# In both expert layers, every block of the first product from block 36 on runs as 512-column matmuls, where every second one did

## The chip, the cores and the metric

The kernel runs on one core of one Trainium2 chip. The metric is the device time of one execution in microseconds (us), the median over several runs. Engines are named as in the profile: PE is TensorE's matmul, PEld its weight load, DVE is VectorE, ACT is ScalarE, POOL is GpSimd, SP is SyncE.

## The reference

A model of three layers, on 256 tokens of width 1024, in float32: a layer of retention and a layer of differential attention, each followed by an expert layer (`peer_ffn`), and then a third layer with a gated recurrence and two feed-forward parts. The change touches the two expert layers only. For a token, 8 heads choose 16 experts each out of 16384 by two sets of 128 keys; of each chosen expert a row of `u` is multiplied with the token, and the weighted gelu of it with a row of `v`:

```python
u_e = jnp.take(u, idx, axis=0)
v_e = jnp.take(v, idx, axis=0)
act = jax.nn.gelu(jnp.einsum('ted,td->te', u_e, xc).astype(jnp.float32))
return jnp.einsum('te,ted->td', (gate * act).astype(v_e.dtype), v_e)
```

## The kernel before

The kernel doesn't gather experts. `peer` computes the first product for all 16384 of them, in 128 blocks (`i2`) of 128 experts by 256 tokens, takes gelu of it into a tile H, multiplies H with gates that are zero but for the chosen experts, and multiplies H with all of `v`. It runs twice, once a layer.

Products are made exact enough by splitting: each operand becomes a high and a low float32r half, and three of the four products are summed. Of x the two halves lie side by side in one tile, `both`, with 256 columns each. Weights come by DMA on SP's queue in pieces of 128 x 1024 (`stream`), four in flight, and `split` turns a piece into `wh` (ScalarE, line 124) and `wl` (VectorE, line 125), with three buffers of each and high priority. So for every block ScalarE and VectorE do one long split, about two blocks ahead of its use.

There are two ways to compute a block. `gemm_a` makes 24 matmuls of 256 columns (lines 146 to 148): for each of 8 slices of the width, high weights by high x, high weights by low x, low weights by high x, all into the same 256 columns of a PSUM bank. `gemm_ab` makes 16 (lines 158 to 162): high weights by both halves of x at once, 512 columns, and low weights by high x, 256 columns. That leaves two partial results side by side in the bank. ScalarE copies the right one to `lo` (line 1246), VectorE adds the two into `su` (line 1247), and gelu then reads `su` instead of the bank. `lo` and `su` lie in `parts`, a tile with two places for each.

PSUM has eight banks here: two for blocks (`s.mm`), two for transposes and scores (`s.aux`), four for gates (`s.acc`). So a block can start when the block before the last one has left its bank.

Blocks 0 to 35 (`K0` is 36) run beside the routing, which VectorE does; they all use `gemm_a`. From block 36 on the gates are made as well, 64 groups of 4 tokens spread over the blocks: VectorE builds two one-hot tiles for a group (lines 1452 and 1453; the second is written into one of two places, so it waits for the group before the last one), PE multiplies them in 8 short f16 matmuls (line 1464), and VectorE and ScalarE apply the result to H (lines 1469 and 1472). Once gates have been applied to some tokens, the gelu of later blocks goes to a tile of its own for these tokens, and VectorE multiplies it into H (lines 1260 and 1261). From block 36 on even blocks use `gemm_ab` and odd blocks `gemm_a`.

Nobody writes the order of the instructions on an engine by hand: a planner orders them before the run by readiness and priority over the whole program, and each engine then follows its list strictly in that order.

After block 127 the second product follows: for each `i2` ScalarE and VectorE split a row of H into `gh` and `gl`, and PE multiplies (line 1286).

Of the kernel before, what the change touches and what calls it, by code (L numbers as in the profile page):

```python
# [49 lines left out]
K0 = 36  # L50
# [17 lines left out]
class Ker:  # L68
# [1095 lines left out]
    def peer(s, l, xs, units_q, units_u, units_v, ln):  # L1164
        nc, A = s.nc, s.A
        with ExitStack() as cx:
# [14 lines left out]
            parts = xs[0].rearrange("p (b a t) -> p b a t", b=2, a=2)  # L1181
# [34 lines left out]
            def scores(c):  # L1216
                ps = s.aux()[:, :T].rearrange("p (a b) -> p a b", a=2)
                for tt in range(2):
                    nc.tensor.matmul(ps[:, tt], qT[:, c, tt * 128:tt * 128 + 128], sk[:, c], start=True, stop=True)
                nc.scalar.activation(sc[:, :, c], ps, AF.Copy)  # L1220
# [15 lines left out]
            pend = []  # L1236
            for i2 in range(NKEYS):
                ps = s.mm()
                if i2 < K0 or i2 % 2:
                    ps = ps[:, :T]  # L1240
                    s.gemm_a(next(units_u), xT, ps)
                else:

                    s.gemm_ab(next(units_u), both, ps)
                    lo, su = (parts[:, i2 // 2 % 2, j] for j in range(2))
                    nc.scalar.activation(lo, ps[:, T:], AF.Copy)
                    nc.vector.tensor_tensor(su, ps[:, :T], lo, op=ALU.add)
                    ps = su
                if i2 < 2:
                    if i2 == 0:  # L1250
                        scores(15)
                    s.route_keys(rt, sc, 14 + i2)
                nt = 4 * g
                if nt == 0:
                    nc.scalar.activation(H[:, i2], ps, AF.Gelu_apprx_tanh)
                else:
                    if nt < T:
                        nc.scalar.activation(H[:, i2, nt:], ps[:, nt:], AF.Gelu_apprx_tanh)
                    ge = po.tile([128, T], F32, name="gelu")
                    nc.scalar.activation(ge[:, :nt], ps[:, :nt], AF.Gelu_apprx_tanh)  # L1260
                    nc.vector.tensor_tensor(H[:, i2, :nt], H[:, i2, :nt], ge[:, :nt], op=ALU.mult)
                if 2 <= i2 < K0:
                    for _ in range(ROUTE_STEPS):
                        next(route, None)
                    if i2 == K0 - 1:
                        for _ in route:
                            pass
                elif i2 >= K0:
                    for f in pend:
                        f(i2 + 1)  # L1270
                        g += 1
                    e = (i2 + 2 - K0) * (T // 4) // (NKEYS - KEND - K0)
                    pend = [s.gates(H, s.onehots(po, rt, j), j) for j in range(g, min(e, T // 4))]
# [391 lines left out]
```

## Time and profile before

| | |
|---|---|
| median of 3 runs | 2709.18 us (2705.35 to 2709.56) |
| the profiled execution, its time | 2703.24 us |
| the profiled execution, its span | 2701.4 us |
| mean granted TensorE clock | 0.996 |
| PE busy | 2660.6 us (98%) |
| PEld busy | 2326.7 us (86%) |
| DVE busy | 1955.8 us (72%) |
| ACT busy | 1427.8 us (53%) |

The profile shows one execution. Its span goes from the first to the last instruction; its time is measured from outside and is 1.8 us longer. Busy shares are of the span. Matmuls overlap and their ends are modelled, so the share of PE says little by itself; the starts of matmuls are what can be relied on.

### The profile page before, as it was taken

The numbers are of one execution on the slowest core, as the hardware profiler recorded it, in microseconds if no ns is written. First come the engines' busy times: TensorE is split into PE (matmuls) and PEld (weight loads), VectorE is DVE, ScalarE is ACT, GpSimd is POOL, SyncE is SP. The second block draws the span as 40 slices with busy tenths as digits, with TensorE's granted clock in tenths as the row PEclk, the third lists the DMA queues.
The fourth block names the chain that finished last, engine by engine and source line by source line (L and its number), as shares of the span: only waits on it lengthen the run. The fifth ranks groups of instructions, "written<-read, shape, count | busy, mean of one in ns | idle before, by whom it ended". The sixth has DMA issues, their size and how long they took to land. (4 is left out here: it accounts for less than half of the span.)

```text
span 2701.4 us, 43500 instructions
## 1 busy us (share of the span) xinstructions
PE 2660.6 (98%) x16326; PEld 2326.7 (86%) x16326; DVE 1955.8 (72%) x3668; ACT 1427.8 (53%) x2553; POOL 12.3 (0%) x32
## 2 busy tenths in 40 slices
PE   9999999999999999999999999999999999999999
PEld 7789999999888888799999998888878887888887
DVE  7558978888666668689788886666687576665774
ACT  4445555555555555555555555555555474443554
POOL 0000000000000000000000000000000000000000
PEclk9999999999999999999999999999999999999999
DMA  6455555545666664355555556565655543122554
GB/s 211 153 185 183 180 172 168 168 165 190 200 194 195 193 195 151 102 181 179 174 165 166 169 179 210 192 193 194 195 169 189 188 161 110 56 71 78 172 187 148
DMA packets 125570, 454.65 MB, mean 168 GB/s; under 512 B 14464, under 2 KB 15248, under 8 KB 125104
## 3 DMA queue, kind: packets, MB, share of 16 engines
q1 hardware_dynamic: 124064, 447.62, 50.9%
q0 software_dynamic: 1152, 4.19, 0.4%
q8 instruction: 128, 2.10, 0.3%
q14 instruction: 82, 0.67, 0.1%
q10 hardware_dynamic: 144, 0.07, 0.0%
HBM read 448.66 MB, written 3.15 MB: 167 GB/s over the span
## 5 line engine op out<-in xcount | busy, mean ns | idle before, releaser
L125 DVE TENSOR_TENSOR wl<-raw,wh 128x1024 fp32r<-128x1024 f32 x830 | 1014.5, 1223 | 429.2 <-ACT wh L124 427.5
L124 ACT ACTIVATE wh<-raw 128x1024 fp32r<-128x1024 f32 x830 | 879.4, 1060 | 736.0 <-issue 198.9
L146 PE MATMUL mm<-xT,wh 128*128 128x256 f32 x1648 | 468.7, 285 | 3.2 <-ACT ge L258 2.3
L148 PE MATMUL mm<-xT,wl 128*128 128x256 f32 x1648 | 465.8, 283 | 1.8 <-DVE wl L125 1.8
L147 PE MATMUL mm<-xT,wh 128*128 128x256 f32 x1648 | 467.1, 284 | 0.0
L158 PE MATMUL mm<-xT,wh 128*128 128x512 f32 x1050 | 381.0, 402 | 0.8 <-ACT wh L124 0.6
L147 PEld LDWEIGHTS mm<-xT,wh 128*128 128x128 f32 x1648 | 314.6, 191 | 5.0 <-DVE xT L260 0.3
L146 PEld LDWEIGHTS mm<-xT,wh 128*128 128x128 f32 x1648 | 314.2, 191 | 5.4 <-ACT ge L258 2.7
L1286 PE MATMUL acc<-wl,gh 128*128 128x512 f32 x1024 | 317.4, 389 | 0.3
L148 PEld LDWEIGHTS mm<-xT,wl 128*128 128x128 f32 x1648 | 314.7, 191 | 2.6 <-DVE wl L125 2.4
L1286 PE MATMUL acc<-wh,gl 128*128 128x512 f32 x1024 | 316.6, 389 | 0.0
L159 PE MATMUL mm<-xT,wl 128*128 128x256 f32 x1050 | 292.5, 279 | 0.8 <-DVE wl L125 0.8
L1286 PE MATMUL acc<-wh,gh 128*128 128x512 f32 x1024 | 277.8, 389 | 2.8 <-ACT gh L1295 2.8
L1295 ACT ACTIVATE gh<-H 128x256 fp32r<-128x256 f32 x256 | 106.5, 417 | 297.4 <-PE acc L1286 297.4
L158 PEld LDWEIGHTS mm<-xT,wh 128*128 128x128 f32 x1050 | 197.1, 188 | 42.1 <-DVE qk_u L169 1.3
L1286 PEld LDWEIGHTS acc<-wh,gh 128*128 128x128 f32 x1024 | 192.0, 188 | 43.0 <-ACT gh L1295 3.2
L1286 PEld LDWEIGHTS acc<-wl,gh 128*128 128x128 f32 x1024 | 192.2, 188 | 41.1 <-DVE wl L125 1.1
L1286 PEld LDWEIGHTS acc<-wh,gl 128*128 128x128 f32 x1024 | 192.1, 188 | 39.9
L159 PEld LDWEIGHTS mm<-xT,wl 128*128 128x128 f32 x1050 | 197.7, 188 | 3.4 <-DVE wl L125 1.1
L1296 DVE TENSOR_TENSOR gl<-H,gh 128x256 fp32r<-128x256 f32 x256 | 108.4, 425 | 114.7 <-PE acc L1286 114.7
L1453 DVE TENSOR_TENSOR x<-o,slotG 128x1024 f16<-128x1024 f16 x128 | 88.3, 689 | 45.3 <-PE acc L1464 45.2
L158 PE MATMUL aux<-xT,wh 128*128 128x512 f32 x294 | 105.1, 394 | 0.0
(544 smaller groups left out, 3929.9 us busy)
## 6 DMA issues: line engine op xcount, KB each, us to landing
raw<-peer_u SPq DMA_DIRECT2D x256, 512.0 KB, 3.6
raw<-peer_v SPq DMA_DIRECT2D x256, 512.0 KB, 4.4
raw<-ffn_w SPq DMA_DIRECT2D x132, 512.0 KB, 4.2
raw<-peer_q SPq DMA_DIRECT2D x32, 512.0 KB, 3.8
raw<-ret_qk SPq DMA_DIRECT2D x16, 512.0 KB, 3.5
raw<-ret_v SPq DMA_DIRECT2D x16, 512.0 KB, 3.8
raw<-ret_g SPq DMA_DIRECT2D x16, 512.0 KB, 3.7
raw<-ret_o SPq DMA_DIRECT2D x16, 512.0 KB, 3.2
```

Of the source, the lines that this page charges most:

```text
L124: a = nc.scalar.activation(h, ap, AF.Copy)
L125: d = nc.vector.tensor_tensor(l, ap, h.bitcast(F32), op=ALU.subtract)
L146: nc.tensor.matmul(out, w[0][:, c], x[0][:, d], start=start and d == 0, stop=False)
L147: nc.tensor.matmul(out, w[0][:, c], x[1][:, d], start=False, stop=False)
L148: nc.tensor.matmul(out, w[1][:, c], x[0][:, d], start=False, stop=stop and d == ND - 1)
L158: nc.tensor.matmul(ps, w[0][:, c], x, start=d == 0, stop=False)
L159: nc.tensor.matmul(ps[:, :T], w[1][:, c], both[:, d, 0], start=False, stop=False)
L1286: mm = nc.tensor.matmul(accs[cb][tt], a[:, t], b[:, cb * 512:cb * 512 + 512], start=i2 == 0 and wi == 0, stop=i2 == NKEYS - 1 and wi == 2)
L1295: a = nc.scalar.activation(wh, H[:, i2], AF.Copy).ins
L1296: d = nc.vector.tensor_tensor(wl, H[:, i2], wh.bitcast(F32), op=ALU.subtract).ins
L1453: nc.vector.tensor_tensor(v(og), o[:, :, 1:2].to_broadcast([128, 4, 2, 128]), tok(rt["G"]), op=ALU.mult)
```

## The change

Both ways stay as they are. The condition that chooses between them loses its second half, so odd blocks from 36 on use `gemm_ab` too, and the place in `parts` follows the block's number instead of half of it: a place is used again after two blocks, where it was used again after four.

```diff
             for i2 in range(NKEYS):
                 ps = s.mm()
-                if i2 < K0 or i2 % 2:
+                if i2 < K0:
                     ps = ps[:, :T]
                     s.gemm_a(next(units_u), xT, ps)
                 else:
 
                     s.gemm_ab(next(units_u), both, ps)
-                    lo, su = (parts[:, i2 // 2 % 2, j] for j in range(2))
+                    lo, su = (parts[:, i2 % 2, j] for j in range(2))
                     nc.scalar.activation(lo, ps[:, T:], AF.Copy)
                     nc.vector.tensor_tensor(su, ps[:, :T], lo, op=ALU.add)
                     ps = su
```

## Rows read from the trace of the kernel before

**Rows 1.** The page, part 1: busy time and instructions of the engines.

```profile
PE 2660.6 (98%) x16326; PEld 2326.7 (86%) x16326; DVE 1955.8 (72%) x3668; ACT 1427.8 (53%) x2553; POOL 12.3 (0%) x32
```

**Rows 2.** Windows, first expert stage: busy us and instructions by engine, clock, DMA.

```profile
core 0: us, PE busy (x) PEld busy (x) DVE busy (x) ACT busy (x) POOL busy (x), PEclk, DMA share, GB/s
380.00:450.00 70.00, 70.00 (x561) 65.60 (x560) 53.62 (x96) 39.52 (x90) 0.00 (x0) 1.00 0.51 166
520.00:590.00 70.00, 70.00 (x571) 65.70 (x571) 61.58 (x104) 37.40 (x94) 0.00 (x0) 1.00 0.50 166
```

**Rows 3.** Timeline of PE, first expert stage: start, us, engine, line, operands.

```profile
499.77 0.28 PE L146 MATMUL mm<-xT,wh 128*128 128x256 f32 x1
...
502.63 1.07 PE L1464 MATMUL acc<-x,o 128*128 128x128 f16 x16
503.51 0.47 PE L158 MATMUL mm<-xT,wh 128*128 128x512 f32 x1
...
506.13 0.40 PE L162 MATMUL mm<-xT,wh 128*128 128x512 f32 x1
506.37 0.28 PE L146 MATMUL mm<-xT,wh 128*128 128x256 f32 x1
...
509.23 0.62 PE L1464 MATMUL acc<-x,o 128*128 128x128 f16 x8
509.66 0.47 PE L158 MATMUL mm<-xT,wh 128*128 128x512 f32 x1
```

**Rows 4.** Timeline of PE, second feed-forward part: starts of two successive blocks.

```profile
2019.90 0.39 PE L158 MATMUL mm<-xT,wh 128*128 128x512 f32 x1
...
2022.69 0.39 PE L158 MATMUL aux<-xT,wh 128*128 128x512 f32 x1
```

**Rows 5.** Groups by line, whole span; then the timeline's first and last gate cluster.

```profile
L1464 PE MATMUL acc<-x,o 128*128 128x128 f16 x1024 | 74.2, 220 | 0.0
...
L1247 DVE TENSOR_TENSOR x<-mm,x 128x256 f32<-128x256 f32 x92 | 38.4, 417 | 0.0
...
388.75 0.62 PE L1464 MATMUL acc<-x,o 128*128 128x128 f16 x8
...
648.63 1.07 PE L1464 MATMUL acc<-x,o 128*128 128x128 f16 x16
```

**Rows 6.** Timeline of ACT and DVE behind a 16-matmul block; idle time in brackets.

```profile
506.56 1.06 ACT L124 ACTIVATE wh<-raw 128x1024 fp32r<-128x1024 f32 x1 [2.02 <-PE mm L162]
507.53 0.37 ACT L1246 ACTIVATE x<-mm 128x256 f32<-128x256 f32 x1
...
507.66 1.23 DVE L125 TENSOR_TENSOR wl<-raw,wh 128x1024 fp32r<-128x1024 f32 x1 [0.17 <-ACT wh L124]
508.80 0.42 DVE L1247 TENSOR_TENSOR x<-mm,x 128x256 f32<-128x256 f32 x1
```

**Rows 7.** Timeline of PE, then of DVE, behind a 24-matmul block with gates.

```profile
591.78 0.28 PE L148 MATMUL mm<-xT,wl 128*128 128x256 f32 x1
...
592.57 0.69 DVE L1453 TENSOR_TENSOR x<-o,slotG 128x1024 f16<-128x1024 f16 x1 [0.49 <-PE acc L1464]
593.17 0.69 DVE L1452 TENSOR_TENSOR o<-iota,slotI 128x1024 f16<-128x1024 f16 x1
593.78 1.22 DVE L125 TENSOR_TENSOR wl<-raw,wh 128x1024 fp32r<-128x1024 f32 x1
594.91 0.58 DVE L1469 SCALAR_TENSOR_TENSOR H<-acc,H 128x412 f32<-128x412 f32 x1
```

**Rows 8.** Timeline of DVE and PE near the end of the stage, no gates between.

```profile
654.79 0.42 DVE L1247 TENSOR_TENSOR x<-mm,x 128x256 f32<-128x256 f32 x1
...
655.11 0.28 PE L148 MATMUL mm<-xT,wl 128*128 128x256 f32 x1
655.26 0.50 PE L158 MATMUL mm<-xT,wh 128*128 128x512 f32 x1
```

**Rows 9.** Windows late in the first and in the second expert stage.

```profile
605.00:635.00 30.00, 30.00 (x244) 28.09 (x240) 28.16 (x46) 15.67 (x42) 0.00 (x0) 1.00 0.49 161
1550.00:1590.00 40.00, 40.00 (x326) 37.51 (x325) 37.17 (x60) 20.30 (x52) 0.00 (x0) 1.00 0.49 162
```

**Rows 10.** Timeline of PE where the second product begins; idle time in brackets.

```profile
668.41 0.73 PE L1286 MATMUL acc<-wh,gh 128*128 128x512 f32 x2 [1.38 <-ACT gh L1295]
```

## The prediction

> **What bounds the kernel now.** I read the page first: TensorE is busy for 2660.6 of 2701.4 us [rows 1]. A busy share is a modelled figure, so I went on to the stretches that the change touches. In each of the two expert stages (one per layer) block 36 of the first product starts near 380 us and 1330 us and the last ends near 667 us and 1616 us. There, by windows, PE is busy all the time at a granted clock of 1.00; VectorE is busy for 53.62 of 70 us early and 61.58 of 70 us later, ScalarE for little over half, the DMA engines for half [rows 2]. PE sets the pace, and VectorE is the engine that comes up behind it. The work is static per engine, so the next view is the timeline of PE, read by the starts of first matmuls, since ends of matmuls are modelled.
>
> Two kinds of block alternate. A 24-matmul block runs from 499.77 to 502.63, 2.86 us; then one or two groups of gate products (8 short f16 matmuls, 0.43 us a group: 509.23 to 509.66); then a 16-matmul block from 503.51 to 506.37, also 2.86 us [rows 3]. Both stream the same 6144 columns. So at first sight the change wins nothing. But the second figure holds a switch: this block comes straight after gate products. In the later feed-forward stage the same 16 matmuls follow one another with nothing between, and the pitch is 2.79 us (2019.90 to 2022.69) [rows 4]. The difference, 0.07 us, is what a block pays for coming behind f16 gate products.
>
> **The change, part by part.** There are 92 sums on VectorE in the old kernel [rows 5], 46 a layer; the change adds 46 a layer.
>
> *TensorE.* A converted block comes behind another 16-matmul block and goes from 2.86 to 2.79 us: 0.07 us each, 92 of them, so 6.4 us saved. That is the ceiling of the gain, 0.24%. The Trainium skill (TensorE: Matmul & The Clock Gate, section on the back-to-back issue gap) gives a column count over 2.4 GHz plus 2.5 ns as the pitch; by that an estimate is 2.62 against 2.60 us, and the whole saving 1.9 us. The rows decide here: 24 matmuls in 2.86 us are 119 ns each, not 109, so I keep 6.4.
>
> *The gate products.* There are 1024 gate matmuls, 8 a group, so 64 groups a layer [rows 5]. In the trace they stand behind 24-matmul blocks only: counted on PE's timeline of the first layer's stage, 42 clusters with 60 groups (4 run earlier), one or two in each, the first at 388.75, the last at 648.63 [rows 5]. My reading: a 16-matmul block can't start before its PSUM bank is free, which takes long (below), and gates that are ready slip in ahead of it; a 24-matmul block's bank was emptied by ScalarE and it is ready early. With all blocks alike, gates slip in ahead of any, up to 60 clusters. That is 18 more switches a layer of 0.07 us, 2.5 us for both. Bounds: 0 if the clusters stay, 2.5 if not. I take 2.5.
>
> *The bank.* This is the costly part. The mm pool has two banks, so block n+2 needs the bank of block n. Follow a 16-matmul block: its last matmul ends at 506.53 (506.13 + 0.40) [rows 3]. ScalarE first splits a weight block (506.56, 1.06 us), then copies the low half (507.53); VectorE subtracts for the same split (507.66, 1.23 us) and only then adds (508.80, 0.42 us) [rows 6]. The bank is free 2.69 us after the end. Where no gates lie between, that is already too late: VectorE's sum ends at 655.21, and the next 16-matmul block starts at 655.26, right behind it, though the last matmul before it started 0.15 us earlier at 655.11 and the next is due after 0.12 [rows 8]. The old kernel lives with this since a cluster of gates stands in nearly every pair.
>
> Now the converted blocks. Behind a block that gates follow, VectorE does other work first: 591.78 + 0.28 ends such a block at 592.06; at 592.57 comes the second one-hot product, which waits for the gates, at 593.17 the next one-hot comparison, at 593.78 the weight subtraction, and the slot after it opens at 594.91 [rows 7]. If the new sum takes that slot, the bank is free at 594.91 + 0.42, 3.27 us after the end, and PE can start 0.05 later. PE wants it, if one group of gates lies between, at 0.43 + 2.86 − 0.16 = 3.13 us after the end (0.16 is the part of the last matmul that overlaps the next start). So PE waits 0.19 us. With gates on both sides of the next block it wants it 0.43 later and doesn't wait; with none behind the block the sum is at 2.69 and doesn't wait either. The 92 blocks of a layer meet 60 groups, so 32 gaps are without gates, some 28 of them (an estimate, all but the first and last few blocks) behind a block with gates: 28 × 0.19 × 2 = 10.6 us.
>
> Bounds: 0, if VectorE's order puts the sum ahead of the one-hots. Above, VectorE is behind when the block ends: a gated block is a subtraction, a sum, two one-hots, one gate application and one gelu product, by starts in [rows 7] and [rows 6] about 1.14 + 0.34 + 0.60 + 0.61 + 0.5 + 0.3 = 3.5 us against 3.29 us of PE; after two in a row the lag is 0.4 us, the wait 0.4, and the term 22 us. I take 10.6, since the rows show one-hots ahead of the subtraction each time gates precede.
>
> *VectorE as such.* It needs 0.34 us more a pair (its rows overlap by some 80 ns, so 0.42 counts as 0.34), 0.55 us in 10 us. Over 605 to 635 us it is busy for 28.16 of 30 us, over 1550 to 1590 for 37.17 of 40 [rows 9]: 94% and 93%, and 99% with the sums. There its order, with waits for the gates and for ScalarE in it, has no room. I put 0.1 us on each of the last 25 blocks, 5 us for both layers; bounds 0 and 10.
>
> *ScalarE* gets 0.37 us a block and is about half idle [rows 2]: nothing, but at the end. There PE waits 1.38 us for the first split of H (668.41), which ScalarE does [rows 10]; the last block's copy, 0.37 us as at 507.53 [rows 6], can come ahead of it: 0.35 us, 0.7 for both layers. If it comes behind, 0.
>
> *DMA* transfers are unchanged; the engines are half idle [rows 2], and a pace faster by 1% asks nothing of them. The halves' places are used again after two blocks, 5.6 us, instead of four; gelu, their only reader besides the sum, is done by then: nothing.
>
> Sum: −6.4 + 2.5 + 10.6 + 5 + 0.7 = +12.4 us. The profiled execution took 2703.24 us, so 2715.6. It was 5.9 us below the median of the runs, 2709.18; by that median the forecast is 2721.6, and I say 2722.
>
> **The rivals.** *Faster.* The sum is queued ahead of the one-hots behind every block and the gates stay in clusters, so no bank is late: −6.4 + 0.7 = −5.7, 2703. For it: the old order already puts the sum right behind the subtraction [rows 6]. Against: behind gates the one-hots are ready at 0.5 us and the subtraction only at 1.1 us, when its ScalarE half is done. It decides whether the bank is free by 3.08 us after the end. The Trainium skill (Perfetto Trace Analysis, section on optimizing tensor performance) holds with this side: larger matmuls are more efficient, and rotating banks overlaps emptying with the next group. The trace agrees only while gates lie between: without them the overlap is used up already [rows 8]. Chance 0.2.
>
> *A wash.* The sum comes early, gates spread: −6.4 + 2.5 + 0.7 = −3.2 and 0 to 4 for VectorE late: about −1.2, 2708. Chance 0.3. That the change saves nothing on PE at all, since the columns are the same, and no bank is late, ends here too.
>
> *VectorE sets the pace* in most of the stage: blocks in a row with gates cost 3.5 us and idle time before the one-hots adds up (0.49 us at 592.57 [rows 7]). Bank term 22, late term 10: −6.4 + 2.5 + 22 + 10 + 0.7 = +29, 2738, or more. Against: over the early window VectorE has 16 of 70 us free [rows 2]. Chance 0.12.
>
> The forecast has 0.38; its own range, with 0.10 to 0.30 us for the wait and 2 to 8 for the late part, is 2714 to 2731.
>
> **How the numbers follow.** Cases of both signs hold much, so the range goes from the faster rival to the slow one, 2703 to 2738. 0.2%, 5.4 us, is about what a measurement of this kernel tells from no change. The faster rival barely passes it: with those of the wash that reach it, 0.17. Slower: nearly all of the forecast and the slow rival, 0.48. Within: 0.35.
>
> **What would show it.** Right: in the new profile PE idles, or the start-to-start of a 16-matmul block exceeds 2.86 us, where gates precede but don't follow the block before; those starts lie 0.05 us behind the end of a sum; gates stand behind even and odd blocks; the sum comes third behind two one-hot instructions. Wrong: a pair of blocks takes 5.65 us plus gates throughout, with sums ending at 2.69 us. Also wrong, and not seen here: the order is planned anew over the whole program, and a shift far from the expert stages could move the time by as much.

## The result, and the profile after

The changed kernel takes 2724.25 us in the median of 6 runs (2719.04 to 2727.02), the kernel before 2708.76 us in 6 runs (2705.35 to 2711.38). The ratio is 1.0058, 95% interval 1.0048 to 1.0068: 15.5 us slower, where 2722 was forecast. The number came out close, but the sum behind it did not: its largest term was less than half of what the traces show, two others were too large, and something that it didn't hold, the clock, gave some 8 us back.

The profiled execution took 2722.17 us, its span is 2720.4 us. On the page, busy time and instructions have moved as the change says: 736 matmuls fewer than in [rows 1] (8 in each of 92 blocks), 92 more instructions on VectorE and on ScalarE.

```profile
PE 2668.7 (98%) x15590; PEld 2282.9 (84%) x15590; DVE 1987.8 (73%) x3760; ACT 1461.1 (54%) x2645; POOL 12.4 (0%) x32
```

Where the time went is seen first in the windows of the first expert stage, and late in both stages (columns as in [rows 2]). PE, which was busy for 70.00 of 70 us, now is for 68.5, and VectorE is no busier in the middle of the stage than before, 61.57 against 61.58 us. It was not VectorE that ran full: PE stopped, and everything else with it. That holds late in the stages too, against [rows 9].

```profile
520.00:590.00 70.00, 68.51 (x464) 57.87 (x463) 61.57 (x111) 40.22 (x101) 0.00 (x0) 1.00 0.48 159
605.00:635.00 30.00, 29.40 (x197) 24.99 (x196) 27.87 (x47) 16.70 (x44) 0.00 (x0) 1.00 0.49 163
1550.00:1590.00 40.00, 39.39 (x272) 33.40 (x272) 36.53 (x62) 22.14 (x56) 0.00 (x0) 1.00 0.47 159
```

The length of a stage is read on PE's timeline, from the first matmul of the first 16-matmul block to the first of the second product. First the changed kernel, layer by layer, then the kernel before (its 668.41 is in [rows 10]):

```profile
377.10 0.40 PE L158 MATMUL mm<-xT,wh 128*128 128x512 f32 x1
...
679.53 0.73 PE L1286 MATMUL acc<-wh,gh 128*128 128x512 f32 x2 [1.72 <-ACT gh L1295]
...
1337.32 0.40 PE L158 MATMUL mm<-xT,wh 128*128 128x512 f32 x1
...
1640.22 0.50 PE L1286 MATMUL acc<-wh,gh 128*128 128x512 f32 x1 [1.72 <-ACT gh L1295]
```

```profile
377.32 0.40 PE L158 MATMUL mm<-xT,wh 128*128 128x512 f32 x1
...
1327.03 0.40 PE L158 MATMUL mm<-xT,wh 128*128 128x512 f32 x1
...
1618.13 0.73 PE L1286 MATMUL acc<-wh,gh 128*128 128x512 f32 x2 [1.38 <-ACT gh L1295]
```

The stages took 291.1 us each (668.41 − 377.32, 1618.13 − 1327.03) and take 302.4 and 302.9: 23.1 us more. The span is only 19.0 us longer, the median of the runs 15.5. The rest is TensorE's clock outside the stages. The trace of before has a stretch at half of it (1.2 instead of 2.4 GHz; granted 0.50 from 1130 to 1135 us) between the two stages, that of after has none there; the windows of the one and of the other:

```profile
1125.00:1137.00 12.00, 10.74 (x46) 7.88 (x46) 6.94 (x22) 6.20 (x26) 0.00 (x0) 0.72 0.26 87
```

```profile
1125.00:1180.00 55.00, 50.95 (x262) 38.92 (x261) 36.99 (x79) 29.31 (x70) 1.08 (x2) 1.00 0.40 141
```

It is so in the runs too: the mean granted clock is 0.9973 over the six of after (0.995 to 0.999) and 0.9946 over 29 of before (0.993 to 0.996), taken with the first experiments. Multiply each run's time by its granted clock, so that half speed counts half, and after has 2716.5 us in the mean, before 2692.7: 23.8 us apart, as the stages say. Below this is called the clock-corrected time. It is an estimate, for it treats the whole program as if TensorE set its pace. Why the clock falls less often in the changed kernel no run here shows.

What happens in the stage is what the prediction described. PE's timeline has the starts of blocks and gates:

```profile
523.15 0.40 PE L162 MATMUL mm<-xT,wh 128*128 128x512 f32 x1
523.39 0.62 PE L1464 MATMUL acc<-x,o 128*128 128x128 f16 x8
523.82 0.48 PE L158 MATMUL mm<-xT,wh 128*128 128x512 f32 x1
...
526.96 0.47 PE L158 MATMUL mm<-xT,wh 128*128 128x512 f32 x1
...
532.87 0.40 PE L162 MATMUL mm<-xT,wh 128*128 128x512 f32 x1
533.11 1.07 PE L1464 MATMUL acc<-x,o 128*128 128x128 f16 x16
533.99 0.48 PE L158 MATMUL mm<-xT,wh 128*128 128x512 f32 x1
...
537.28 0.47 PE L158 MATMUL mm<-xT,wh 128*128 128x512 f32 x1 [0.26 <-DVE x L1247]
537.59 0.28 PE L159 MATMUL mm<-xT,wl 128*128 128x256 f32 x1
```

VectorE's timeline has what stands between the end of the block ahead of the gates and the sum that empties its bank:

```profile
524.05 0.69 DVE L1453 TENSOR_TENSOR x<-o,slotG 128x1024 f16<-128x1024 f16 x1 [0.58 <-PE acc L1464]
524.66 0.68 DVE L1452 TENSOR_TENSOR o<-iota,slotI 128x1024 f16<-128x1024 f16 x1
525.26 1.22 DVE L125 TENSOR_TENSOR wl<-raw,wh 128x1024 fp32r<-128x1024 f32 x1
526.40 0.42 DVE L1247 TENSOR_TENSOR x<-mm,x 128x256 f32<-128x256 f32 x1
...
533.77 0.69 DVE L1453 TENSOR_TENSOR x<-o,slotG 128x1024 f16<-128x1024 f16 x1 [0.33 <-PE acc L1464]
534.38 1.28 DVE L1452 TENSOR_TENSOR o<-iota,slotI 128x1024 f16<-128x1024 f16 x2
535.59 1.22 DVE L125 TENSOR_TENSOR wl<-raw,wh 128x1024 fp32r<-128x1024 f32 x1
536.72 0.41 DVE L1247 TENSOR_TENSOR x<-mm,x 128x256 f32<-128x256 f32 x1
```

The first case has one group of gates. The block ends at 523.55 (523.15 + 0.40), its sum at 526.82, 3.27 us later, and the block that wants the bank starts at 526.96. The block between took 3.14 us instead of 2.86. The second case has two groups. The block ends at 533.27, three one-hot instructions come first, the sum ends at 537.13, 3.86 us later; PE starts at 537.28, and the block between took 3.29 us. Counted on PE's timeline of the first layer, 30 blocks are of this kind (gates ahead of them, none behind), 3.22 us on average, and behind 28 of them the next block starts 0.14 to 0.15 us after the end of a sum; the 15 with gates on both sides take 2.88. Of the 60 groups of gates there are still only 45 clusters, against 42 before.

### The profile page after: what moved, and what is told of

It reads as the page before. It is cut to its first block, busy times and chain, and to the rows that moved or that the text cites. A ratio compares the mean times of both kernels' runs of the same rounds, so it can differ in the third digit from the quotient of the medians.

```text
span 2720.4 us, 42273 instructions
## 1 busy us (share of the span) xinstructions
PE 2668.7 (98%) x15590; PEld 2282.9 (84%) x15590; DVE 1987.8 (73%) x3760; ACT 1461.1 (54%) x2645; POOL 12.4 (0%) x32
## 5 line engine op out<-in xcount | busy, mean ns | idle before, releaser
L158 PE MATMUL mm<-xT,wh 128*128 128x512 f32 x1694 | 617.8, 403 | 12.0 <-DVE x L1247 8.0
L159 PE MATMUL mm<-xT,wl 128*128 128x256 f32 x1694 | 474.8, 280 | 0.8 <-DVE wl L125 0.8
L158 PEld LDWEIGHTS mm<-xT,wh 128*128 128x128 f32 x1694 | 318.1, 188 | 96.2 <-PE mm L162 26.8
L159 PEld LDWEIGHTS mm<-xT,wl 128*128 128x128 f32 x1694 | 320.3, 189 | 4.4 <-DVE wl L125 1.1
L146 PE MATMUL mm<-xT,wh 128*128 128x256 f32 x912 | 263.0, 290 | 3.2 <-ACT ge L258 2.3
L148 PE MATMUL mm<-xT,wl 128*128 128x256 f32 x912 | 260.3, 286 | 1.8 <-DVE wl L125 1.8
L147 PE MATMUL mm<-xT,wh 128*128 128x256 f32 x912 | 261.2, 287 | 0.0
L146 PEld LDWEIGHTS mm<-xT,wh 128*128 128x128 f32 x912 | 175.7, 193 | 5.4 <-ACT ge L258 2.7
L148 PEld LDWEIGHTS mm<-xT,wl 128*128 128x128 f32 x912 | 176.2, 193 | 2.7 <-DVE wl L125 2.4
L147 PEld LDWEIGHTS mm<-xT,wh 128*128 128x128 f32 x912 | 176.2, 193 | 0.6 <-DVE xT L260 0.3
```

Of the source, the lines that this page charges most:

```text
L146: nc.tensor.matmul(out, w[0][:, c], x[0][:, d], start=start and d == 0, stop=False)
L147: nc.tensor.matmul(out, w[0][:, c], x[1][:, d], start=False, stop=False)
L148: nc.tensor.matmul(out, w[1][:, c], x[0][:, d], start=False, stop=stop and d == ND - 1)
L158: nc.tensor.matmul(ps, w[0][:, c], x, start=d == 0, stop=False)
L159: nc.tensor.matmul(ps[:, :T], w[1][:, c], both[:, d, 0], start=False, stop=False)
```

## The experiments

Each ratio below is to the kernel before on the same chip in the same session (medians 2706.75 to 2707.28 us of 21 to 29 runs).

**A third bank** (three_banks). The changed kernel with three banks for these products and one auxiliary bank instead of two and two.

```
-            s.psum(cx, 2, 2, 4)
+            s.psum(cx, 3, 1, 4)
```

> The changed kernel with three PSUM banks for blocks instead of two and one for scores and transposes instead of two. Bank theory (TensorE waits since the sum that empties the bank stands behind two one-hot instructions and a subtraction on VectorE, and block n+2 needs that bank): block n+3 needs it now, the waits of 0.28 to 0.43 us that stand before 30 blocks of each layer are gone, and what is left is the saving of 0.07 us a block, less a few more switches: 2702 to 2706 us, 0.998 to 0.999 of the kernel before. Load theory (VectorE has simply too much to do): VectorE's work is the same, so TensorE still waits, for weights or gates instead, and the time stays near 2720 us, 1.004 or more.

Measured: 2711.15 us, ratio 1.0019 (1.0010 to 1.0028), more than the bank theory's range and well under the load theory's. Most of the loss is gone though nothing was said of VectorE's order, and so are PE's waits for the sum. The stage takes 293.8 us in either layer. Of the 2.7 us above before's 291.1, some 1.3 are gate matmuls that ran ahead of the stage there (505 in the stage, 480 before, at 0.43 us for 8). Nor do shorter blocks show, since the planner now cuts the gates up; PE's timeline has pieces of groups behind nearly every block (88 changes from gates to blocks in the stage, 45 in the changed kernel):

```profile
503.39 0.51 PE L1464 MATMUL acc<-x,o 128*128 128x128 f16 x6
...
509.87 0.40 PE L1464 MATMUL acc<-x,o 128*128 128x128 f16 x4
```

**ScalarE empties the bank** (scalar_empties). In the changed kernel ScalarE copies all 512 columns, and the sum is made from SBUF, so that no bank waits for VectorE.

```
-                    lo, su = (parts[:, i2 % 2, j] for j in range(2))
-                    nc.scalar.activation(lo, ps[:, T:], AF.Copy)
-                    nc.vector.tensor_tensor(su, ps[:, :T], lo, op=ALU.add)
+                    su, lo = (parts[:, i2 % 2, j] for j in range(2))
+                    nc.scalar.activation(parts[:, i2 % 2].rearrange("p a t -> p (a t)"), ps, AF.Copy)
+                    nc.vector.tensor_tensor(su, su, lo, op=ALU.add)
```

> The changed kernel, but ScalarE copies all 512 columns of the bank to the two places of the sum, and VectorE adds from there. VectorE's work is the same, only that it no longer holds the bank. Bank theory: the bank is free some 1.0 + 0.6 us after a block's end instead of 3.3 or more, no block waits, 2702 to 2706 us, 0.998 to 0.999 of the kernel before. Load theory: near 2720 us, 1.004 or more.

Measured: 2711.05 us, ratio 1.0017 (1.0008 to 1.0026), again between the two expectations and far nearer to the bank theory's; stages of 292.3 us. VectorE has as many instructions as in the changed kernel, and no wait of PE for the sum is left. So the loss is the bank's, not the additional sums' own time. PE's timeline shows here what a converted block is worth:

```profile
500.33 0.62 PE L1464 MATMUL acc<-x,o 128*128 128x128 f16 x8
500.75 0.48 PE L158 MATMUL mm<-xT,wh 128*128 128x512 f32 x1
501.07 0.28 PE L159 MATMUL mm<-xT,wl 128*128 128x256 f32 x1
...
503.66 0.40 PE L158 MATMUL mm<-xT,wh 128*128 128x512 f32 x1
503.89 0.28 PE L159 MATMUL mm<-xT,wl 128*128 128x256 f32 x1
...
506.48 0.62 PE L1464 MATMUL acc<-x,o 128*128 128x128 f16 x8
```

Behind another block it takes 2.82 us (503.66 to 506.48), behind gates 2.91; the difference is in the first interval, 0.32 against 0.23 us. Here all 60 groups stand by themselves, 60 changes a stage.

**The load without the bank, first try** (sum_without_bank). The kernel before, with a ScalarE copy and a VectorE sum more in each odd block, from SBUF to SBUF; their result is not used. They write to the second place of `parts`, so the even blocks keep to the first (here and in the two later runs of the load).

```
+                    if i2 >= K0:
+                        nc.scalar.activation(parts[:, 1, 0], both[:, 0, 0].bitcast(F32), AF.Copy)
+                        nc.vector.tensor_tensor(parts[:, 1, 1], both[:, 0, 1].bitcast(F32), parts[:, 1, 0], op=ALU.add)
...
-                    lo, su = (parts[:, i2 // 2 % 2, j] for j in range(2))
+                    lo, su = (parts[:, 0, j] for j in range(2))
```

> The kernel before, with odd blocks as 24 matmuls, plus one more copy on ScalarE and one more sum on VectorE for each odd block, both from SBUF and to SBUF and read by nobody (they add nothing to the result). So VectorE and ScalarE have the work of the changed kernel, TensorE and the banks that of the kernel before. Bank theory: nothing waits for them, 0.999 to 1.002 of the kernel before. Load theory: 1.004 or more, as in the changed kernel.

Measured: 2721.02 us, ratio 1.0055 (1.0043 to 1.0067). Taken by itself this looks like the load theory. The trace says that the run doesn't test it: the additional sums depend on nothing, and the planner put them ahead of the stage. VectorE has 186 instructions between 300 and 350 us where before has 110, and in the stage no more than before (58.62 against 58.98 us from 450 to 520). Their price is paid once a layer, where the routing comes late and the blocks at the start of the stage wait; windows, then PE's first waits in the first stage, from 377 to 400 us (us in total, times, longest; another of 2.5 us follows at 401.57, and two of 3.4 and 0.9 us come in the second stage):

```profile
300.00:350.00 50.00, 49.76 (x415) 49.52 (x414) 47.52 (x186) 29.96 (x52) 0.00 (x0) 1.00 0.57 181
450.00:520.00 70.00, 70.00 (x571) 65.68 (x571) 58.62 (x104) 38.71 (x93) 0.00 (x0) 1.00 0.50 165
```

```profile
PE mm L146 <- DVE x L1250: 2.9, 1, 2.9
PE mm L158 <- ACT gelu L1263: 1.7, 1, 1.7
```

**The third bank in the kernel before** (three_banks_alternating). The same line as in the first experiment, in the kernel before.

> Control for the three banks: the kernel before with three banks for blocks and one for scores and transposes. Both theories expect no more than the few waits without gates gone, 0.998 to 1.001 of the kernel before. If it comes out slower, the bank taken from scores and transposes has a price of its own, and the three-bank version of the change is to be read against this one.

Measured: 2711.83 us, ratio 1.0016 (1.0007 to 1.0025). A third bank costs the old kernel 0.16%, about what the changed kernel with three banks is behind. Read against this control, the changed kernel with three banks has the shorter stages, 293.8 against 295.3 us. Gates stand behind blocks of both kinds (70 changes to and 70 from gates in the first stage, 42 in the kernel before), and a 24-matmul block behind gates takes 2.95 us. In 13 places of the stage a 16-matmul block comes straight behind a 24-matmul block, and no bank is late; PE's timeline of one:

```profile
408.08 0.28 PE L148 MATMUL mm<-xT,wl 128*128 128x256 f32 x1
408.20 0.40 PE L158 MATMUL mm<-xT,wh 128*128 128x512 f32 x1
408.43 0.28 PE L159 MATMUL mm<-xT,wl 128*128 128x256 f32 x1
```

Its first interval is 0.23 us, in all 13: this change of kind costs nothing.

**The load, second try** (sum_behind_block). The kernel before; from the first gates on, the additional copy and sum of an odd block are queued behind that block's own activation.

```
-                    nc.scalar.activation(ge[:, :nt], ps[:, :nt], AF.Gelu_apprx_tanh)
+                    gl = nc.scalar.activation(ge[:, :nt], ps[:, :nt], AF.Gelu_apprx_tanh)
+                    if i2 % 2:
+                        with s.after(gl.ins):
+                            nc.scalar.activation(parts[:, 1, 0], both[:, 0, 0].bitcast(F32), AF.Copy)
+                            nc.vector.tensor_tensor(parts[:, 1, 1], both[:, 0, 1].bitcast(F32), parts[:, 1, 0], op=ALU.add)
```

> The kernel before, in which each odd block from the first gates on gets one more ScalarE copy and one more VectorE addition of 256 columns, from SBUF to SBUF, queued behind that block's activation; no PSUM bank hangs on them, and their result is not used. It adds the engine load of the change without its wait for a bank. Bank theory (the loss comes from TensorE waiting for a bank that a late sum holds): the blocks keep 2.86 us and the ratio to the kernel before is 0.999 to 1.002 (2706 to 2714 us). Load theory (VectorE and ScalarE have too much to do, and everything behind them comes later): most of the change's loss is there, ratio 1.004 or more (2719 us or more).

Measured: 2722.06 us, ratio 1.0054 (1.0041 to 1.0068). By the number the bank theory has lost here. By the trace the load is now where it should be (62.32 against 58.98 us from 450 to 520), nearly all blocks keep their 2.86 us and the last block of a stage begins 1.4 us later in it than before. Then the additional work of the last blocks stands ahead of the first split of H, PE waits 3.74 us instead of 1.38 (from 668.05 to 671.79), and from the second half of that wait on the granted clock is at its lower level; windows, then PE's timeline:

```profile
670.00:677.00 7.00, 5.21 (x12) 4.18 (x13) 2.39 (x7) 1.45 (x4) 0.54 (x1) 0.51 0.76 225
```

```profile
671.79 1.22 PE L1290 MATMUL acc<-wh,gh 128*128 128x512 f32 x2 [3.74 <-ACT gh L1299]
```

The mean granted clock of its runs is 0.9916, of before's 0.9945; the clock-corrected time is 6.3 us above before's. The loss is at the end of the stage and in the clock, if the trace is read rightly; so the same was run without those last blocks.

**The load, but for the last eight blocks** (sum_behind_block_but_the_last).

```
-                    if i2 % 2:
+                    if i2 % 2 and i2 < NKEYS - 8:
```

> As sum_behind_block, but without the extra copies and additions of the last eight blocks, so that the first activations and splits of the second product have nothing more ahead of them than in the kernel before. In sum_behind_block the blocks kept their pace within about 1 us a layer, and the time went at the end of the stage: TensorE waited 3.7 us for gh instead of 1.4, and the mean granted clock of the runs was 0.9916 instead of 0.9945. Bank theory: with the end cleared the load costs nothing that can be measured, ratio 0.999 to 1.0015, and the granted clock is back at 0.994 to 0.996. Load theory: the extra work on VectorE and ScalarE costs wherever it stands, ratio 1.004 or more.

Measured: 2707.99 us, ratio 0.9997 (0.9987 to 1.0006). The load in the stage is that of sum_behind_block, and the loss is gone; windows, then PE's only wait from 376 to 690 us:

```profile
450.00:520.00 70.00, 70.00 (x571) 65.69 (x570) 62.32 (x115) 41.95 (x105) 0.00 (x0) 1.00 0.51 166
```

```profile
PE acc L1290 <- ACT gh L1299: 1.3, 1, 1.3
```

Part of that is the clock, which was granted at 0.9963, a little above before's; the clock-corrected time is 4.6 us longer. On PE's timeline each stage is 1.1 us longer. Work on VectorE and ScalarE that holds no bank thus costs 2 to 5 us of 24.

**The order on VectorE** (hots_behind_sum). The changed kernel; the one-hots of an iteration are queued behind its sum (`sm` is the sum's instruction). Banks and amount of work are those of the changed kernel.

```
-                    pend = [s.gates(H, s.onehots(po, rt, j), j) for j in range(g, min(e, T // 4))]
+                    with s.after(sm.ins):
+                        hots = [s.onehots(po, rt, j) for j in range(g, min(e, T // 4))]
+                    pend = [s.gates(H, oh, j) for j, oh in enumerate(hots, g)]
```

> The changed kernel, with the one-hot instructions that an iteration issues held back on VectorE until that iteration's sum is done; the amount of work is the same. Order theory (the sum holds its bank longer because one-hots stand ahead of it on VectorE): the sum ends some 2.7 us behind the end of its matmuls instead of 3.2, the block behind a gate group starts without a wait, each layer's stage takes 286 to 291 us instead of 302, and the time is 2702 to 2712 us, ratio 0.998 to 1.002. Load theory: the same work takes the same time, ratio 1.004 to 1.008 (2719 to 2730 us).

Measured: 2706.12 us, ratio 1.0001 (0.9991 to 1.0010). The order alone takes the loss away, or nearly: the clock was granted at 0.9957 here and at 0.9945 in before, and the clock-corrected time is 3.5 us longer than before's. VectorE's timeline behind a block that ends at 502.54 (502.15 + 0.39), with gates behind it:

```profile
503.67 1.23 DVE L125 TENSOR_TENSOR wl<-raw,wh 128x1024 fp32r<-128x1024 f32 x1 [1.18 <-ACT wh L124]
504.81 0.42 DVE L1247 TENSOR_TENSOR x<-mm,x 128x256 f32<-128x256 f32 x1
505.14 0.68 DVE L1454 TENSOR_TENSOR o<-iota,slotI 128x1024 f16<-128x1024 f16 x1
```

The bank is free at 505.23, 2.69 us after the end, the figure of [rows 6]. In the whole stage PE waits 0.2 us for a sum. The stage takes 295.4 us, not the 286 to 291 that were expected; about 1.7 us of that are four groups of gates that ran ahead of it in the kernel before. It doesn't become faster than before: the 64 groups stand singly, 64 changes where before has 42 and the changed kernel 45.

**Fewer changes, by issuing gates at odd blocks only** (scalar_empties_paired_gates and three_banks_paired_gates). The same edit in scalar_empties and in three_banks:

```
+                    e = min(e, T // 4) if i2 % 2 else g
-                    pend = [s.gates(H, s.onehots(po, rt, j), j) for j in range(g, min(e, T // 4))]
+                    pend = [s.gates(H, s.onehots(po, rt, j), j) for j in range(g, e)]
```

> The scalar_empties kernel (ScalarE copies all 512 columns out of the bank, VectorE adds from SBUF) with the gates of a step issued at odd blocks only, two or three groups at a time, so that there are half as many changes between gate weights and block weights. If a change of weights costs 0.07 us and nothing waits, some 15 to 30 changes fewer a layer give 2 to 4 us: 2706 to 2710 us, ratio 0.999 to 1.001. If the larger groups of gates make VectorE late for the next block (the wait comes back), the ratio is 1.002 or more.

> The three_banks kernel with the gates of a step issued at odd blocks only. In three_banks nearly every block had gates ahead of it, and the price of those changes took back the shorter blocks. If that is its whole loss, halving them (87 to about 45 gaps with gates, 42 changes a layer at 0.07 us, two layers: 5.9 us) gives 2704 to 2708 us, ratio 0.998 to 1.000. If the planner cuts the groups up again whatever their issue, the ratio stays at 1.001 to 1.003.

Measured: 2707.42 us, ratio 0.9996 (0.9987 to 1.0005), and 2709.23 us, 1.0006 (0.9997 to 1.0015). The first is better than its parent by 0.2%, the second by 0.1%, which its interval doesn't set apart; and not as meant: the planner cuts the larger batches up, with pieces of 2 to 6 matmuls among them, and the first still has 67 changes a stage (its parent 60), the second 74 (its parent 88). For the first, what made it faster is open.

**Gates in whole pairs** (scalar_empties_two_by_two). In scalar_empties the 16 matmuls of two groups are queued behind a block, and the next block behind them. s.block and s.gate are the last matmul of the block and of the gates.

```
+                    w = next(units_u)
+                    with s.after(s.gate):
+                        s.gemm_ab(w, both, ps)
...
+                    if i2 == K0:
+                        hots = [s.onehots(po, rt, j) for j in range(2)]
+                    if min((i2 + 2 - K0) * (T // 4) // (NKEYS - KEND - K0), T // 4) >= g + 2:
+                        with s.after(s.block):
+                            pend = [s.gates(H, hots[j], g + j) for j in range(2)]
+                        if g + 2 < T // 4:
+                            hots = [s.onehots(po, rt, j) for j in range(g + 2, g + 4)]
```

> The scalar_empties kernel with the gates always in whole pairs of groups: their matmuls are queued on TensorE behind a block and the next block behind them, so that the planner cannot cut them up. About 31 gaps with gates a layer instead of 60. If the 0.08 us by which the first interval of a block behind gates is longer (0.316 against 0.234 us) is the whole price of a gap, 29 gaps fewer in two layers give 4.6 us: from 1.0017 to 1.0000, 0.9985 to 1.0005. If the fixed place makes TensorE wait for one-hots or for a bank of the gates, the ratio is 1.002 or more.

Measured: 2703.91 us, ratio 0.9988 (0.9978 to 0.9999), 32 whole pairs a stage and no wait but the 1.9 us for the first split of H; the stage takes 292.2 us, with all 64 groups of gates in it (60 in the 291.1 us of before). It is the only version here whose interval stays below 1, and by a hair; the clock-corrected time is 2.4 us shorter than before's, so this is not the clock. It took both repairs, the bank's and the gates', to get 0.1% out of the shorter blocks.

**Whole pairs with VectorE emptying the bank** (hots_behind_sum_two_by_two). The same edit in the changed kernel, each pair of one-hots queued behind the sum of its iteration.

> The changed kernel's own way of emptying a bank (ScalarE half, sum on VectorE from the bank), gates in whole pairs as in scalar_empties_two_by_two, and each pair of one-hots held back behind the sum of its iteration. If the bank is the only thing that the change got wrong, there are no waits for a bank and 31 gaps a layer instead of 64 in hots_behind_sum: 33 x 2 x 0.08 us = 5.3 us less than 1.0001, 0.997 to 0.9995. If four one-hot instructions in a row (2.5 us) make the next sum late again, waits of the first matmul of a block for x of the sum come back and the ratio is 1.001 or more.

Measured: 2742.81 us, ratio 1.0123 (1.0107 to 1.0140). The wait is back, and nearly twice as long. VectorE's and PE's timelines, for a block that ends at 506.39 (505.99 + 0.40):

```profile
505.21 1.28 DVE L1463 TENSOR_TENSOR o<-iota,slotI 128x1024 f16<-128x1024 f16 x2
...
507.31 1.28 DVE L1464 TENSOR_TENSOR x<-o,slotG 128x1024 f16<-128x1024 f16 x2
508.52 1.22 DVE L125 TENSOR_TENSOR wl<-raw,wh 128x1024 fp32r<-128x1024 f32 x1
509.65 0.42 DVE L1251 TENSOR_TENSOR x<-mm,x 128x256 f32<-128x256 f32 x1
```

```profile
508.81 0.39 PE L162 MATMUL mm<-xT,wh 128*128 128x512 f32 x1
...
510.13 0.50 PE L158 MATMUL mm<-xT,wh 128*128 128x512 f32 x1 [0.93 <-DVE x L1251]
```

The pair is queued behind one block's sum, but so long that it stands ahead of the next block's: that sum ends at 510.07, 3.68 us after its block, and PE starts 0.06 us later. Here the block between has no gates behind it, so PE wants the bank earlier and waits longer; 24 of the 26 such blocks in the first stage have their bank late. Beside scalar_empties_two_by_two, with the same gates on PE, the only difference is which engine frees the bank and where the one-hots are queued: 39 us.

## Why the prediction was right, and where its sum was not

*The mechanism of the bank was right.* PE waits at the starts that were named: behind a block with gates ahead of it and none behind it. The sum comes behind the one-hots and the subtraction, and with one group its bank is free 3.27 us after the end, as forecast. Three different cures, one bank more, another engine, another order, each take the waits away and 0.4% to 0.6% off the ratio; in clock-corrected time they leave 4.8, 4.2 and 3.5 us of 23.8. The run that worsened the order on VectorE made the waits worse. The rival, load as such, is left with little by sum_behind_block_but_the_last. The places in `parts`, used again after two blocks, stay so in all three cures, so they are not the cause either.

*The bank term was mis-sized: 10.6 us, measured over 20.* 30 blocks a layer stand so, and 28 of them cause a wait, as many as were estimated; that is in part luck, since the estimate let the groups of gates stand singly. The 30 cost 0.34 us each beyond the 2.88 of a block behind gates that causes no wait, not 0.19: 20.4 us in two layers. Half of the clusters ahead of them have two groups, whose additional one-hot makes the bank 0.6 us later (3.86 us) while PE's own work grows by 0.43; the prediction priced one group only. Its upper bound, 22, came near, but from something else, VectorE falling behind after two gated blocks in a row. And PE starts 0.14 us behind the end of the sum (526.82 to 526.96), not 0.05. Blocks that start behind a wait have a first interval of 0.31 instead of 0.23 us (537.28 to 537.59), some 2 us more, and the 15 blocks between two others take 2.90 instead of 2.82, 2.5 us. Together about 25.

*The saving was mis-sized: 6.4 us, measured about 4.* The pitch of 2.79 us came from a feed-forward part; in this stage a block without a wait takes 2.82 (scalar_empties), 0.04 to 0.05 less than a 24-matmul block, 92 times.

*The switches were not added: 2.5 us, measured 0.5.* The clusters stayed nearly as they were, 45 for 42. The price of one was about right: 0.08 us (2.91 against 2.82 in scalar_empties). The runs without waits show the spread that was forecast: 60, 64 and 88 changes.

*VectorE late: 5 us taken, 2 to 5 measured for the load by itself.* In the changed kernel it cannot be seen apart; VectorE isn't full there, 27.87 of 30 us ([rows 9] has the same window of before).

*The end: 0.7 us, measured 0.7.* PE waits 1.72 us for the first split of H instead of 1.38, twice.

The terms as measured, −4 + 0.5 + 25 + 0.7, give 22 us and the stages 23.1; about one us stays unassigned. The forecast's +12.4 met +15.5 because the clock outside the stages gave back some 8 us that the prediction knew nothing of. So close a number was luck: the sum itself was about half of what the stages show. The prediction's last sentence, a shift far from the stages, allowed for such a thing, but named the planner's order as the cause; whether the order has to do with the clock no run here shows.

## What to carry to other kernels

Before making a PSUM bank wait for one more reader, count from the end of its last matmul to the end of that reader, with everything that stands ahead of it on its engine, for each kind of neighbour in the schedule (no gates, one group, two groups), and compare it with what TensorE has to do meanwhile; the worst common neighbour sets the price, not the mean. A reader late by 0.6 us cost more than all that fewer matmuls could save, and queueing it ahead of work that has time to spare was worth as much as a third bank. When an added or moved instruction depends on nothing, look in the trace where the planner put it before believing a ratio.

## What was not expected of the hardware

In sum_behind_block longer waits of TensorE came with time at the lower clock: with the 3.74 us of idle time that end at 671.79 us the granted clock was 0.51 from 670 to 677 us, and with the same wait in the second layer 0.57 from 1629 to 1633 us; behind 1.38 us in before it stayed at 1.00 (668 to 678 us). That is some 5 us (an estimate: 7 × 0.49 + 4 × 0.43), about as much again as the waits grew, 2.36 us twice. By time and granted clock, some 9 of the 15 us of sum_behind_block are the clock; the rest of the 9 lies elsewhere in the program (in the trace 0.83 from 2250 to 2300 us, where before has 0.93) and has no cause shown here, as the 8 us have none that went the other way in the changed kernel. Two kernels that differ by half a per cent are thus compared better with the clock beside the time.

A 16-matmul block's first interval is 0.31 to 0.32 us instead of 0.23 behind gates, and 0.31 to 0.34 behind a wait for a bank. Behind a 24-matmul block without a wait it is 0.23 (three_banks_alternating). In before such a block has 0.34, but there it starts behind a wait too, 0.05 us after the end of a sum [rows 8]. What gates and a wait have in common isn't settled here.
